# Prompt attention in 32-column tiles, both heads of a pair in one visit

## The chip, the cores and the metric

The kernel runs on one core of a Trainium2 chip. The metric is the device time of one execution in microseconds (us); lower is better. A core has TensorE (PE, with PEld for its weight loads), VectorE (DVE), ScalarE (ACT), GpSimd (POOL) and SyncE (SP), which here issues most DMAs. Matmul results go to PSUM, eight banks in which a [128, 512] fp32 tile fills one; everything else works on SBUF.

## The reference, cut to what matters

One layer of a hybrid decoder, for a prompt of 512 tokens and 8 samples of 4 tokens with the same weights: half a SwiGLU block, a mixer, half a SwiGLU block, a final norm. The mixer projects to queries, keys and values for three dilated attention groups, to a gated convolution and to two gates. What the change touches is the prompt attention, 8 heads of 64 in each group:

```python
GROUPS = ((128, 1), (512, 4), (2048, 16))        # window, dilation
sc = einsum('bdcqhe,bdckhe->bdchqk', qb, kk) * SCALE
sc = where(valid, sc, -inf);  m = max(sc);  p = exp(sc - m);  l = sum(p)
o  = einsum('bdchqk,bdckhe->bdcqhe', p, vv) / l
# the three groups of a head are weighted by a softmax over m + log(l)
```

That weighting equals one softmax over the keys of all three groups together, and so the kernel computes it.

## The kernel before, in words

Activations lie transposed, [128 channels, 544 columns]: 512 prompt and 32 sample tokens in two halves of 272. Each 128x128 weight block is split into a high and a low part in a fast matmul format, so a block is six matmuls into a PSUM tile `mp` (three products, two halves); `run_tiles` walks the tiles and calls `slot` every four blocks, that is every 24 matmuls.

Within a block of 128 query tokens the columns are sorted by token mod 4 into four classes of 32. Group 0 (dilation 1) attends to the same and the previous block (128 columns each); groups 1 and 2 need only keys of the query's own class, 32 per key block.

Work that isn't a projection is put between projection blocks by `slot`: `pe_q` holds generators of which the first gives one step per slot (`v_turn` transposes a value tile, `attention(hp)` does head pair hp), `bg_q` holds convolution steps on VectorE (`ac`, one tap each), given out as long as a planner's clock for VectorE (`clocks`, with the costs of `pe_cost` and `dve_cost`) stays behind that of TensorE. `seq` is the order of the mixer's projections: gated convolution tiles (`gb`, `u`), then q, k, v of one head pair, four times; the attention of a pair is queued when its last value tile is evacuated and runs between the projections of the next pair, the last one between the last four tiles of `seq`.

A step of `attention` before serves one head and one query block: outputs `o` of the step two earlier, transposes `pt` of the probabilities of the step before, scores `s` of its own. The scores of group 0 are matmuls of 64 rows and 128 columns, those of groups 1 and 2 of 64 rows and 32 columns, one per class. Behind them VectorE adds the mask, scales and takes the extreme value (`P<-s,mask`), ScalarE takes the exponential with its sum `L`, TensorE transposes `P`, ScalarE copies to `pT`, and TensorE multiplies with `V`, again full width for group 0 and in 32-column tiles for the others. After both heads `aT` transposes the outputs of a query block back. `S` and `O` are PSUM classes of one bank each, `T` of two, `main` of two tiles of two banks.

Of the kernel before, what the change touches and what calls it, by code (L numbers as in the profile page):

```python
# [23 lines left out]
PACK = [(0, 192), (192, 384), (576, 448), (1024, 512)]  # L24
# [66 lines left out]
def step_kernel(ctx: ExitStack, tc: tile.TileContext, I: dict, O: dict, order: list):  # L91
# [143 lines left out]
    def run_tiles(tiles, lead=1, hooks=None, slack=-500.0):  # L235
# [36 lines left out]
    def v2(t):  # L272
        return t.rearrange("p (h n) -> p h n", h=2)
# [179 lines left out]
    mask = qp.tile([128, 1536], F32, name="mask")  # L453
# [154 lines left out]
    def v_turn(g, hp, t):  # L608
        ps = psum_tile([128, 512], "T", f"vT{g}_{hp}", 2)
        for i in range(4):  # L610
            pe.transpose(ps[:, 128 * i : 128 * i + 128], t[:, 128 * i : 128 * i + 128], ident)
        V[g, hp] = qp.tile([128, 4, 128], F32, tag="V", name=f"V{g}_{hp}", bufs=6)
        act.activation(V[g, hp].rearrange("p a b -> p (a b)"), ps, AF.Copy)
        yield

    def attention(hp):
        units = [(b, h) for b in range(4) for h in range(2)]
        st1, st2 = None, None
        on = {}
        fin = None  # L620
        for step in range(len(units) + 3):
            if fin is not None:
                b = fin
                ps = psum_tile([128, 128], "T", f"aT{hp}_{b}", 2)
                pe.transpose(ps, on[b], ident)
                act.activation(v2(att[hp])[:, b // 2, 128 * (b % 2) : 128 * (b % 2) + 128], ps, AF.Copy)
                fin = None
            if st2 is not None:
                b, h, pT, chunks, L = st2
                o = psum_tile([128, 64], "O", f"o{hp}_{b}_{h}", 1)  # L630
                p0 = 64 * h
                blks = ([b - 1] if b else []) + [b]
                for i, kb in enumerate(blks):
                    pe.matmul(o, pT[:, i, :], V[0, hp][:, kb, p0 : p0 + 64], start=i == 0, stop=False)
                n = 32 * (b + 1)
                for g in (1, 2):
                    ci = len(blks) + g - 1
                    for c in range(4):
                        pe.matmul(o[32 * c : 32 * c + 32, :], pT[:n, ci, 32 * c : 32 * c + 32],
                                  V[g, hp][:n, c, p0 : p0 + 64], start=False, stop=g == 2)  # L640
                if h == 0:
                    on[b] = qp.tile([128, 128], F32, tag="on", name=f"on{hp}_{b}", bufs=2)
                dve.reciprocal(L, L)
                dve.tensor_scalar(out=on[b][:, p0 : p0 + 64], in0=o, scalar1=L, scalar2=None, op0=ALU.mult)
                if h == 1:
                    fin = b
                st2 = None
            if st1 is not None:
                b, h, P, chunks, L = st1
                ps = psum_tile([128, 4, 128], "T", f"pt{hp}_{b}_{h}", 2)  # L650
                pT = qp.tile([128, 4, 128], F32, tag="pT", name=f"pT{hp}_{b}_{h}", bufs=2)
                for i, (off, n) in enumerate(chunks):
                    pe.transpose(ps[:n, i, :], P[:, off : off + n], ident)
                nf = sum(n == 128 for _, n in chunks)
                act.activation(pT[:, :nf], ps[:, :nf], AF.Copy)  # L655
                if nf < len(chunks):
                    n = chunks[-1][1]
                    act.activation(pT[:n, nf : len(chunks)], ps[:n, nf : len(chunks)], AF.Copy)
                st2 = (b, h, pT, chunks, L)
                st1 = None  # L660
            if step < len(units):
                b, h = units[step]
                p0 = 64 * h
                S = psum_tile([128, 512], "S", f"s{hp}_{b}_{h}", 1)
                pos, w = PACK[b]

                def blk(t, kb):
                    return v2(t)[p0 : p0 + 64, kb // 2, 128 * (kb % 2) : 128 * (kb % 2) + 128]

                chunks = []  # L670
                off = 0
                for kb in ([b - 1] if b else []) + [b]:
                    pe.matmul(S[:, off : off + 128], blk(Q[0, hp], b), blk(K[0, hp], kb), start=True, stop=True)
                    chunks.append((off, 128))
                    off += 128
                for g in (1, 2):
                    chunks.append((off, 32 * (b + 1)))
                    for kh in range(b // 2 + 1):
                        nb = min(2, b + 1 - 2 * kh)
                        for c in range(4):  # L680
                            kv = v2(K[g, hp])[p0 : p0 + 64, kh, :256].rearrange("p (b c i) -> p c b i", b=2, c=4)
                            pe.matmul(S[32 * c : 32 * c + 32, off : off + 32 * nb],
                                      blk(Q[g, hp], b)[:, 32 * c : 32 * c + 32], kv[:, c, :nb, :],
                                      start=True, stop=True)
                        off += 32 * nb
                P = qp.tile([128, 512], F32, tag="P", name=f"P{hp}_{b}_{h}", bufs=2)
                mn = qp.tile([128, 1], F32, tag="mn", name=f"mn{hp}_{b}_{h}", bufs=4)
                L = qp.tile([128, 1], F32, tag="L", name=f"L{hp}_{b}_{h}", bufs=4)
                dve.tensor_tensor_reduce(
                    out=P[:, :w], in0=S[:, :w], in1=mask[:, pos : pos + w], scale=-0.125, scalar=BIG,  # L690
                    op0=ALU.add, op1=ALU.min, accum_out=mn)
                act.activation(P[:, :w], P[:, :w], AF.Exp, scale=-1.0, bias=mn, accum_out=L)  # L692
                st1 = (b, h, P, chunks, L)
            yield

# [18 lines left out]
    run_tiles(seq, lead=2, hooks={4: mix_stats})  # L714
# [53 lines left out]
    def sample_keys(hf, res):  # L768
# [8 lines left out]
        S = psum_tile([128, 512], "S", f"sA{hf}", 1)  # L777
# [26 lines left out]
        S = psum_tile([128, 512], "S", f"sB{hf}", 1)  # L804
# [12 lines left out]
    def sample_values(hf, res):  # L817
# [15 lines left out]
        o = psum_tile([128, 512], "O", f"so{hf}", 1)  # L833
# [207 lines left out]
def _constants():  # L1041
# [11 lines left out]
    mask = np.zeros((128, 1536), f)  # L1053
    c, i = np.arange(128) // 32, np.arange(128) % 32
    tok = 4 * i + c
    for b in range(4):
# [5 lines left out]
        n = 32 * (b + 1)  # L1062
# [168 lines left out]
```

## Time and profile before

| | us |
|---|---|
| median of three runs (lowest, highest) | 1498.96 (1498.73, 1500.8) |
| profiled execution | 1497.86 |
| its span | 1496.1 |
| TensorE, VectorE, ScalarE, GpSimd busy | 1467.2, 836.1, 475.4, 320.0 |
| attention of the prompt, first score to last `aT` | 502.4 to 822.0 |

The busy time of TensorE counts overlapping matmuls once; what a piece of work holds of the engine is read from the start of its row to the start of the next one. Line 62 is the helper that records the calls of TensorE, VectorE and GpSimd, so instructions are told apart by their tiles: `mp` the projections, `s`, `pt`, `o`, `aT` the attention, `sA`, `sB`, `so` the sample attention. fp32 matmuls appear as two records each, transposes and `mp` matmuls as one.

### The profile page before, as it was taken

Reading aid. Unit: us, or ns where it says so; the run is one execution under the profiler, and the core shown is the slowest. Engines: PE = TensorE matmul, PEld = TensorE weight load, DVE = VectorE, ACT = ScalarE, POOL = GpSimd, SP = SyncE. Lnnn points to the kernel's source line nnn. Section 1 sums busy time; section 2 is a strip of 40 time slices with the busy share of each in tenths; the row PEclk is TensorE's granted clock in tenths of the full one; section 3 lists DMA queues with packets and bytes.
Section 4 is the critical chain, followed back from the end, with each engine's and each line's share of the span. In section 5 each row is a group of like instructions: output and inputs, shape, how many; then the busy total and the mean of one; then the engine's idle time right before and its main releaser. Section 6 shows DMA issues by size and latency. Waiting matters only on the chain.

```text
span 1496.1 us, 28970 instructions
## 1 busy us (share of the span) xinstructions
PE 1467.2 (98%) x12680; PEld 1418.8 (95%) x12680; DVE 836.1 (56%) x1134; ACT 475.4 (32%) x630; POOL 320.0 (21%) x222
## 2 busy tenths in 40 slices
PE   7999999999999999999999999999999999999996
PEld 7999999999999999999998888789999999999996
DVE  6554445342389879785746866438355544453334
ACT  6222222122353543544444234411332222221221
POOL 1221111101123325332321332103312211110001
PEclk9999999999999999999999999999999999999999
DMA  5444544465598757667572776644443444444331
GB/s 179 183 169 171 181 169 170 178 223 186 175 232 206 171 131 196 143 146 175 124 181 93 263 246 222 201 161 151 149 156 141 142 143 153 142 141 149 133 113 61
DMA packets 63119, 248.67 MB, mean 166 GB/s; under 512 B 8784, under 2 KB 13392, under 8 KB 62160
## 3 DMA queue, kind: packets, MB, share of 16 engines
q1 hardware_dynamic: 54704, 218.71, 41.7%
q0 software_dynamic: 7488, 27.27, 10.9%
q8 instruction: 100, 1.64, 0.4%
q10 hardware_dynamic: 800, 0.84, 0.2%
q14 instruction: 27, 0.22, 0.0%
HBM read 234.21 MB, written 67.10 MB: 201 GB/s over the span
## 4 chain that ended last, share of the span: by engine, by line
PE 92%; DVE 4%; ACT 2%; DMA 1%; issue 0%; POOL 0%; SPq 0%; DVEq 0%; POOLq 0%
PE mp L62 84%; PE s L62 2%; PE o L62 1%; PE mplast L62 1%; PE pt L62 1%; PE so L62 1%; PE sA L62 1%; DVE ga L62 1%; DMA wlo<-in_ws 1%; DVE ac L62 0%; ACT c L927 0%; PE sB L62 0%; PE vT L62 0%; PE st L62 0%; ACT ah L298 0%
## 5 line engine op out<-in xcount | busy, mean ns | idle before, releaser
L62 PE MATMUL mp<-ah,whi 128*128 128x272 f32 x2496 | 526.5, 292 | 6.9 <-ACT whi L166 5.7
L62 PE MATMUL mp<-ah,wlo 128*128 128x272 f32 x2496 | 517.8, 289 | 0.7 <-DMA wlo<-in_ws 0.7
L62 PE MATMUL mp<-al,whi 128*128 128x272 f32 x2496 | 514.6, 287 | 0.1
L62 PEld LDWEIGHTS mp<-ah,whi 128*128 128x128 f32 x2496 | 391.2, 189 | 20.5 <-issue 10.5
L62 PEld LDWEIGHTS mp<-ah,wlo 128*128 128x128 f32 x2496 | 393.7, 189 | 1.3 <-DMA wlo<-in_ws 0.9
L62 PEld LDWEIGHTS mp<-al,whi 128*128 128x128 f32 x2496 | 392.4, 189 | 0.3 <-DVE al L62 0.3
L62 POOL TENSOR_TENSOR wlo<-wraw,whi 128x1024 fp32r<-128x1024 f32 x73 | 177.1, 2427 | 798.4 <-ACT whi L166 488.1
L166 ACT ACTIVATE whi<-wraw 128x1024 fp32r<-128x1024 f32 (+1 forms) x169 | 177.2, 1049 | 346.7 <-PE mp L62 178.4
L62 DVE TENSOR_TENSOR wlo<-wraw,whi 128x1024 fp32r<-128x1024 f32 (+1 forms) x96 | 117.7, 1226 | 221.4 <-ACT whi L166 221.1
L62 DVE SCALAR_TENSOR_TENSOR ac<-u,vec,ac 128x512 f32<-128x512 f32 x232 | 183.3, 848 | 0.0
L348 ACT ACTIVATE ga<-ga 128x544 f32<-128x544 f32 x44 | 29.0, 658 | 237.2 <-DVE ga L62 237.2
L62 DVE TENSOR_TENSOR ga<-ga,mp 128x544 f32<-128x544 f32 x52 | 37.4, 720 | 103.4 <-PE mp L62 101.2
L62 DVE TENSOR_TENSOR ga<-mp,rstd 128x544 f32<-128x544 f32 x52 | 37.6, 724 | 85.5 <-PE mp L62 85.4
L159 ACT ACTIVATE whi<-wraw 128x1024 fp32r<-128x1024 f32 x52 | 54.9, 1055 | 84.4 <-PE mp L62 83.3
L161 POOL DMA_DIRECT2D wlo<-in_ws x52 | 45.6, 877 | 160.6 <-ACT wlo L160 150.9
L160 ACT ACTIVATE wlo<-whi 128x1024 fp32r<-128x1024 f32 x52 | 55.1, 1061 | 1.6
L62 PEld LDWEIGHTS s<-k,q 64*32 64x32 f32 (+1 forms) x880 | 26.1, 117 | 9.9 <-DVE on L62 2.5
L62 DVE CUSTOM_DVE_ANT_0 P<-s,mask 128x192 f32<-128x192 f32 (+3 forms) x32 | 17.7, 554 | 31.3 <-PE s L62 31.2
L62 PE MATMUL s<-k,q 64*32 64x64 f32 (+2 forms) x880 | 34.3, 223 | 0.0
L62 POOL TENSOR_TENSOR q<-q,ra 128x544 f32<-128x544 f32 x12 | 18.6, 1550 | 61.1 <-DVE ra L62 34.7
L692 ACT ACTIVATE P<-P,mn 128x192 f32<-128x192 f32 (+3 forms) x32 | 19.8, 618 | 36.8 <-DVE mn L62 36.7
L62 PE MATMUL o<-V,pT 64*32 64x64 f32 (+4 forms) x624 | 27.5, 230 | 1.0 <-ACT pT L655 1.0
(780 smaller groups left out, 1992.2 us busy)
## 6 DMA issues: line engine op xcount, KB each, us to landing
wraw<-in_ws SPq DMA_DIRECT2D x219, 512.0 KB, 3.4
cache<-in_cache SPq DMA_DIRECT2D x56, 512.0 KB, 4.6
wlo<-in_ws POOLq DMA_DIRECT2D x52, 512.0 KB, 6.3
out_kv<-k SPq DMA_DIRECT2D x12, 272.0 KB, 3.9
out_kv<-vt SPq DMA_DIRECT2D x12, 256.0 KB, 3.9
x<-in_x SPq DMA_DIRECT2D x8, 272.0 KB, 5.6
xkeep<-x SPq DMA_DIRECT2D x8, 272.0 KB, 2.1
xb<-xkeep SPq DMA_DIRECT2D x8, 272.0 KB, 3.3
```

The source lines that it names most:

```text
L62: return f(*a, **kw)
L159: act.activation(whi[u], raw[u], AF.Copy)
L160: act.activation(wlo[u], whi[u].bitcast(F32), AF.Copy, scale=-1.0)
L161: nc.gpsimd.dma_start(wlo[u], I["ws"][u], accum_op=ALU.add)
L166: act.activation(whi[u][:, c], raw[u][:, c], AF.Copy)
L348: act.activation(t, t, AF.Silu)
L692: act.activation(P[:, :w], P[:, :w], AF.Exp, scale=-1.0, bias=mn, accum_out=L)
```

## The change

`attention` now works on both heads of a pair in one step. The scores of all three groups are 64-row, 32-column matmuls; the two heads, which lie in rows 0 to 63 and 64 to 127, alternate, each with its own PSUM tile. Outputs are 32-column matmuls throughout, both heads into one PSUM tile, with one reciprocal and one product. Query blocks 0 and 1 now take 64 keys of groups 1 and 2 (`NCK`, masked beyond the valid ones), so that the two groups fill one operand of 128 rows; a merged value tile `Vm` is made for that by two more copies per pair. Scores of a block stand in one step, the outputs of the block before and the transposes of this one in the next. `S` has two banks and takes the place of `O`. The last four projection tiles of `seq` have a slot every two blocks, and the planner's cost of 32-column matmuls is lower.

```diff
-PACK = [(0, 192), (192, 384), (576, 448), (1024, 512)]
+PACK = [(0, 256), (256, 384), (640, 448), (1088, 512)]
+NCK = [64, 64, 96, 128]
@@ pe_cost
     if out.shape[0] == 32:
-        return (170.0 + 1.5 * n) / 4
+        return max(13.4, 1.67 * n * src.shape[0] / 512)
@@ run_tiles(..., every=4)
-                if k % 4 == 3 or k == n - 1:
+                if k % every == every - 1 or k == n - 1:
                     slot(slack)
@@ v_turn
+        if g:
+            if g == 1:
+                V["m", hp] = qp.tile([128, 4, 128], F32, tag="Vm", name=f"Vm{hp}", bufs=1)
+            r = 64 * (g - 1)
+            act.activation(V["m", hp][r : r + 64].rearrange("p a b -> p (a b)"), ps[:64], AF.Copy)
@@ attention
+        def scores(b):
+            S = [psum_tile([128, 512], "S", f"s{hp}_{b}_{h}", 2) for h in range(2)]
...
+            def tiles(cols, n, g, keys):
+                for c in range(4):
+                    for h in range(2):
+                        r = slice(64 * h, 64 * h + 64)
+                        q0 = HALF * (b // 2) + 128 * (b % 2) + 32 * c
+                        pe.matmul(S[h][32 * c : 32 * c + 32, cols : cols + n], Q[g, hp][r, q0 : q0 + 32],
+                                  keys(K[g, hp][r], c), start=True, stop=True)
...
+            tiles(0, n0, 0, near)
+            off = n0
+            for g in (1, 2):
+                for kh in range(b // 2 + 1):
+                    nb = min(2, NCK[b] // 32 - 2 * kh)
...
+                    tiles(off, 32 * nb, g, far)
+                    off += 32 * nb
+            L[b] = qp.tile([128, 2], F32, tag="L", name=f"L{hp}_{b}", bufs=3)
+            for h in range(2):
...
+                dve.tensor_tensor_reduce(
+                    out=p[:, :w], in0=S[h][:, :w], in1=mask[:, pos : pos + w], scale=-0.125, scalar=BIG,
+                    op0=ALU.add, op1=ALU.min, accum_out=mn)
+                act.activation(p[:, :w], p[:, :w], AF.Exp, scale=-1.0, bias=mn, accum_out=L[b][:, h : h + 1])
...
+        def values(b):
+            o = psum_tile([128, 2, 64], "S", f"o{hp}_{b}", 2)
+            near = [(V[0, hp][:, kb], None) for kb in blocks(b)]
+            far = [(None, V["m", hp])] if NCK[b] == 64 else [(None, V[g, hp]) for g in (1, 2)]
+            parts = near + far
+            for h in range(2):
+                for i, (v, vc) in enumerate(parts):
+                    n = chunks(b)[i][1]
                     for c in range(4):
+                        rhs = (v if vc is None else vc[:n, c])[:, 64 * h : 64 * h + 64]
+                        pe.matmul(o[32 * c : 32 * c + 32, h, :], pT[b, h][:n, i, 32 * c : 32 * c + 32], rhs,
+                                  start=i == 0, stop=i == len(parts) - 1)
...
+        for b in range(6):
+            if b >= 2:
+                final(b - 2)
+            if b < 4:
+                scores(b)
             yield
+            if 1 <= b < 5:
+                values(b - 1)
+            if b < 4:
+                turn(b)
+            if b < 5:
+                yield
@@ behind seq
-    run_tiles(seq, lead=2, hooks={4: mix_stats})
+    run_tiles(seq[:-4], lead=2, hooks={4: mix_stats})
+    run_tiles(seq[-4:], every=2)
@@ sample attention
-        o = psum_tile([128, 512], "O", f"so{hf}", 1)
+        o = psum_tile([128, 512], "S", f"so{hf}", 2)
```

TensorE, first pair, second head of block 0, before: the transposes of the first head (`pt_0_0`), the scores of the second (`s_0_1`), then projection. Shapes are output rows x columns.

```order
L62 MATMUL pt_0_0_5231<-ident,P_0_0_5190 128x128
L62 MATMUL pt_0_0_5231<-ident,P_0_0_5190 32x128 x2
L62 MATMUL s_0_1_5238<-k_0_4532,q_0_4464 128x128
L62 MATMUL s_0_1_5238<-k_0_4747,q_0_4666 32x32 x4
L62 MATMUL s_0_1_5238<-k_0_4967,q_0_4891 32x32 x4
L62 MATMUL mp_5197<-ah_4_3598,whi_5041 128x272 x2
```

The same block's scores after, at the seam between group 0 (`k_0_4532`) and group 1 (`k_0_4747`):

```order
L64 MATMUL s_0_0_5183<-k_0_4532,q_0_4464 32x128
L64 MATMUL s_0_1_5184<-k_0_4532,q_0_4464 32x128
L64 MATMUL s_0_0_5183<-k_0_4747,q_0_4666 32x64
L64 MATMUL s_0_1_5184<-k_0_4747,q_0_4666 32x64
L64 MATMUL s_0_0_5183<-k_0_4747,q_0_4666 32x64
```

The two heads now alternate matmul by matmul, in one tile shape, 24 of them in this block; no transposes stand beside them.

TensorE, first pair, outputs of block 0, before: first head's outputs (`o_0_0`), second head's transposes, first head's scores of block 1.

```order
L62 MATMUL o_0_0_5290<-V_0_4712,pT_0_0_5232 128x64
L62 MATMUL o_0_0_5290<-V_0_4937,pT_0_0_5232 32x64 x4
L62 MATMUL o_0_0_5290<-V_0_5145,pT_0_0_5232 32x64 x4
L62 MATMUL pt_0_1_5303<-ident,P_0_1_5248 128x128
L62 MATMUL pt_0_1_5303<-ident,P_0_1_5248 32x128 x2
L62 MATMUL s_1_0_5310<-k_0_4532,q_0_4464 128x128 x2
L62 MATMUL s_1_0_5310<-k_0_4747,q_0_4666 32x64 x4
L62 MATMUL s_1_0_5310<-k_0_4967,q_0_4891 32x64 x4
```

And after:

```order
L64 MATMUL o_0_5374<-V_0_4712,pT_0_0_5254 32x64 x4
L64 MATMUL o_0_5374<-Vm_4939,pT_0_0_5254 32x64 x4
L64 MATMUL o_0_5374<-V_0_4712,pT_0_1_5259 32x64 x4
L64 MATMUL o_0_5374<-Vm_4939,pT_0_1_5259 32x64 x4
L64 MATMUL pt_1_0_5394<-ident,P_1_0_5331 128x128 x3
L64 MATMUL pt_1_1_5400<-ident,P_1_1_5335 128x128 x3
L64 MATMUL mp_5342<-ah_4_3598,whi_5111 128x272 x2
```

Both heads' outputs stand together, and the transposes behind them are those of the next block, both heads.

ScalarE, last pair, before: the sigmoid of a gate tile (`gb`), weight splits, a value copy, then the first exponential.

```order
L484 ACT_TABLE_LOAD
L484 ACTIVATE gb_8599<-gb_8599 128x544
L159 ACTIVATE whi_8605<-wraw_8488 128x1024
L160 ACTIVATE wlo_8606<-whi_8605 128x1024
L613 ACTIVATE V_3_8641<-vT_3_8636 128x512
L692 ACT_TABLE_LOAD
L692 ACTIVATE P_0_0_8682,L_0_0_8684<-P_0_0_8682,mn_0_0_8683 128x192
```

And after:

```order
L615 ACTIVATE V_3_8664<-vT_3_8659 128x512
L621 ACTIVATE Vm_8515<-vT_3_8659 64x512
L486 ACT_TABLE_LOAD
L486 ACTIVATE gb_8679<-gb_8679 128x544
L675 ACT_TABLE_LOAD
L675 ACTIVATE P_0_0_8710,L_0_8709<-P_0_0_8710,mn_0_0_8711 128x256
L675 ACTIVATE P_0_1_8714,L_0_8709<-P_0_1_8714,mn_0_1_8715 128x256
```

The attention begins one projection tile earlier, so that the two exponentials stand right behind the sigmoid.

## Rows read from the trace of the kernel before

**Rows 1.** The page of the kernel before: span, two engines, the chain by engine.
```profile
span 1496.1 us, 28970 instructions
...
PE 1467.2 (98%) x12680; PEld 1418.8 (95%) x12680; DVE 836.1 (56%) x1134; ACT 475.4 (32%) x630; POOL 320.0 (21%) x222
...
PE 92%; DVE 4%; ACT 2%; DMA 1%; issue 0%; POOL 0%; SPq 0%; DVEq 0%; POOLq 0%
```
**Rows 2.** Windows, second pair's attention: length, busy PE, PEld, DVE, ACT, POOL, clock, DMA.
```profile
600.00:646.00 46.00, 46.00 (x607) 41.87 (x605) 32.93 (x77) 22.00 (x44) 11.92 (x13) 1.00 0.60 134
```
**Rows 3.** PE timeline, first pair, blocks 0 and 1: start, length, instruction, count.
```profile
502.01 0.41 PE L62 MATMUL mp<-al,whi 128*128 128x272 f32 x2
502.35 0.74 PE L62 MATMUL s<-k,q 64*128 64x128 f32 x18
503.02 0.52 PE L62 MATMUL mp<-ah,whi 128*128 128x272 f32 x2
...
510.34 0.69 PE L62 MATMUL o<-V,pT 128*128 128x64 f32 x18
510.96 0.55 PE L62 MATMUL pt<-ident,P 128*128 128x128 f32 x3
511.44 1.07 PE L62 MATMUL s<-k,q 64*128 64x128 f32 x20
512.43 0.52 PE L62 MATMUL mp<-ah,whi 128*128 128x272 f32 x2
```
**Rows 4.** PE timeline, first pair, block 2.
```profile
520.97 0.91 PE L62 MATMUL o<-V,pT 128*128 128x64 f32 x20
521.81 0.65 PE L62 MATMUL pt<-ident,P 128*128 128x128 f32 x4
522.40 1.19 PE L62 MATMUL s<-k,q 64*128 64x128 f32 x36
523.52 0.52 PE L62 MATMUL mp<-ah,whi 128*128 128x272 f32 x2
```
**Rows 5.** PE timeline, last pair, block 3.
```profile
809.93 1.29 PE L62 MATMUL s<-k,q 64*128 64x128 f32 x36
811.15 0.52 PE L62 MATMUL mp<-ah,whi 128*128 128x272 f32 x2
```
**Rows 6.** PE timeline, a visit of the sample attention in 32-column tiles.
```profile
844.83 1.07 PE L62 MATMUL sB<-cache,qbd 128*32 128x512 f32 x8
845.83 0.52 PE L62 MATMUL mp<-ah,whi 128*128 128x272 f32 x2
846.18 0.42 PE L62 MATMUL mp<-ah,wlo 128*128 128x272 f32 x2
846.44 0.42 PE L62 MATMUL mp<-al,whi 128*128 128x272 f32 x2
```
**Rows 7.** PE timeline, end of the last pair; idle time and releaser in brackets.
```profile
820.39 1.02 PE L62 MATMUL o<-V,pT 128*128 128x64 f32 x20 [1.02 <-ACT pT L655]
822.03 0.33 PE L62 MATMUL aT<-ident,on 128*128 128x128 f32 x1 [0.62 <-DVE on L62]
```
**Rows 8.** ACT timeline, first pair, a gate tile's sigmoid between two exponentials.
```profile
511.35 1.28 ACT L484 ACT_TABLE_LOAD   x1 [3.03 <-DVE L L62]
512.64 0.66 ACT L484 ACTIVATE gb<-gb 128x544 f32<-128x544 f32 x1
...
513.74 1.28 ACT L692 ACT_TABLE_LOAD   x1
515.03 0.62 ACT L692 ACTIVATE P<-P,mn 128x384 f32<-128x384 f32 x1
```
**Rows 9.** The tiles s and P: engine, operation, count, duration ns min/median/max.
```profile
L62 PEld LDWEIGHTS s<-k,q x880: 102/107/188, 502.3 to 816.7; 64*32 64x32 f32 x160, 64*128 64x128 f32 x16
...
L62 DVE CUSTOM_DVE_ANT_0 P<-s,mask x32: 331/590/693, 503.5 to 817.0; 128x192 f32<-128x192 f32 x8, 128x384 f32<-128x384 f32 x8, 128x448 f32<-128x448 f32 x8, 128x512 f32<-128x512 f32 x8
L692 ACT ACTIVATE P<-P,mn x32: 456/644/728, 503.9 to 817.8; 128x192 f32<-128x192 f32 x8, 128x384 f32<-128x384 f32 x8, 128x448 f32<-128x448 f32 x8, 128x512 f32<-128x512 f32 x8
```

More of the change, by code (lines that the diff above doesn't have):

```diff
@@ L233, in mm_block, with run_tiles @@
                 )
-    def run_tiles(tiles, lead=1, hooks=None, slack=-500.0):
+    def run_tiles(tiles, lead=1, hooks=None, slack=-500.0, every=4):
         def new():
@@ L452, in step_kernel @@
     sinr = rope_p.tile([128, NTOK], F32, name="sinr")
-    mask = qp.tile([128, 1536], F32, name="mask")
+    mask = qp.tile([128, 1600], F32, name="mask")
     sp.dma_start(cosr, I["rope"][:, 0])
@@ L611, in v_turn @@
             pe.transpose(ps[:, 128 * i : 128 * i + 128], t[:, 128 * i : 128 * i + 128], ident)
[L612 removed]
+        V[g, hp] = qp.tile([128, 4, 128], F32, tag="V", name=f"V{g}_{hp}", bufs=5)
         act.activation(V[g, hp].rearrange("p a b -> p (a b)"), ps, AF.Copy)
+        if g:
[3 more added lines that the diff above has]
+            act.activation(V["m", hp][r : r + 64].rearrange("p a b -> p (a b)"), ps[:64], AF.Copy)
@@ L614, in v_turn @@
         yield
     def attention(hp):
[L617 to L637, printed above, removed]
-                    for c in range(4):
[L639 to L693, printed above, removed]
-            yield
@@ new lines, in attention, with blocks, chunks, near @@
+        P, pT, L, on = {}, {}, {}, {}
+        def blocks(b):
+            return ([b - 1] if b else []) + [b]
+        def chunks(b):
+            o = 128 * len(blocks(b))
+            r = [(128 * i, 128) for i in range(len(blocks(b)))]
+            n = NCK[b]
+            return r + ([(o, 2 * n)] if n == 64 else [(o, n), (o + n, n)])
+        def scores(b):
+            S = [psum_tile([128, 512], "S", f"s{hp}_{b}_{h}", 2) for h in range(2)]
+            pos, w = PACK[b]
+            n0 = 128 * len(blocks(b))
+            def tiles(cols, n, g, keys):
[5 more added lines that the diff above has]
+                                  keys(K[g, hp][r], c), start=True, stop=True)
+            def near(k, c):
+                if b == 2:
+                    return k[:, 128:416].rearrange("p (a n) -> p a n", a=2)[:, :, :128]
+                k0 = HALF * (b // 2)
+                return k[:, k0 : k0 + n0]
+            tiles(0, n0, 0, near)
[3 more added lines that the diff above has]
+                    nb = min(2, NCK[b] // 32 - 2 * kh)
+                    def far(k, c):
+                        return v2(k)[:, kh, :256].rearrange("p (b c i) -> p c b i", b=2, c=4)[:, c, :nb, :]
+                    tiles(off, 32 * nb, g, far)
+                    off += 32 * nb
+            L[b] = qp.tile([128, 2], F32, tag="L", name=f"L{hp}_{b}", bufs=3)
+            for h in range(2):
+                p = P[b, h] = qp.tile([128, 512], F32, tag="P", name=f"P{hp}_{b}_{h}", bufs=2)
+                mn = qp.tile([128, 1], F32, tag="mn", name=f"mn{hp}_{b}_{h}", bufs=4)
+                dve.tensor_tensor_reduce(
+                    out=p[:, :w], in0=S[h][:, :w], in1=mask[:, pos : pos + w], scale=-0.125, scalar=BIG,
+                    op0=ALU.add, op1=ALU.min, accum_out=mn)
+                act.activation(p[:, :w], p[:, :w], AF.Exp, scale=-1.0, bias=mn, accum_out=L[b][:, h : h + 1])
@@ new lines, in turn @@
+        def turn(b):
+            for h in range(2):
+                ps = psum_tile([128, 4, 128], "T", f"pt{hp}_{b}_{h}", 2)
+                t = pT[b, h] = qp.tile([128, 4, 128], F32, tag="pT", name=f"pT{hp}_{b}_{h}", bufs=2)
+                for i, (off, n) in enumerate(chunks(b)):
+                    pe.transpose(ps[:n, i, :], P[b, h][:, off : off + n], ident)
+                nf = sum(n == 128 for _, n in chunks(b))
+                act.activation(t[:, :nf], ps[:, :nf], AF.Copy)
+                if nf < len(chunks(b)):
+                    n = chunks(b)[-1][1]
+                    act.activation(t[:n, nf : len(chunks(b))], ps[:n, nf : len(chunks(b))], AF.Copy)
@@ new lines, in values @@
+        def values(b):
[3 more added lines that the diff above has]
+            parts = near + far
+            for h in range(2):
+                for i, (v, vc) in enumerate(parts):
+                    n = chunks(b)[i][1]
+                    for c in range(4):
+                        rhs = (v if vc is None else vc[:n, c])[:, 64 * h : 64 * h + 64]
+                        pe.matmul(o[32 * c : 32 * c + 32, h, :], pT[b, h][:n, i, 32 * c : 32 * c + 32], rhs,
+                                  start=i == 0, stop=i == len(parts) - 1)
+            dve.reciprocal(L[b], L[b])
+            on[b] = qp.tile([128, 128], F32, tag="on", name=f"on{hp}_{b}", bufs=2)
+            dve.tensor_tensor(out=on[b].rearrange("p (h e) -> p h e", h=2), in0=o,
+                              in1=L[b].unsqueeze(2).to_broadcast([128, 2, 64]), op=ALU.mult)
@@ new lines, in final @@
+        def final(b):
+            ps = psum_tile([128, 128], "T", f"aT{hp}_{b}", 2)
+            pe.transpose(ps, on[b], ident)
+            act.activation(v2(att[hp])[:, b // 2, 128 * (b % 2) : 128 * (b % 2) + 128], ps, AF.Copy)
+        for b in range(6):
[3 more added lines that the diff above has]
+                scores(b)
+            yield
+            if 1 <= b < 5:
[4 more added lines that the diff above has]
+                yield
```

8 lines of the change are left out of this document (4 added, 4 removed).

## The prediction

> **What bounds the kernel now.** I read the page first. TensorE is busy for 1467 of 1496 us and the chain that ended last lies on it for 92%, while VectorE is busy for 56% [rows 1]; so a microsecond taken from TensorE's own queue is a microsecond of the end, as long as nothing else becomes late. The second view is the stretch of one head pair's attention: TensorE is busy for all of its 46 us, its weight loads for 41.87, VectorE for 32.93, and the granted clock is 1.00, that is 2.4 GHz [rows 2]. The third view is TensorE's timeline there. The attention stands in small visits between groups of 24 matmuls of the input projection (`mp`), and the difference between the start of a row and the start of the next one is what the visit holds of the engine; the length in the row is longer, since matmuls overlap. By this measure a score visit of one head costs 0.67 us for query block 0 and 0.99 for block 1 [rows 3], 1.12 for block 2 [rows 4] and 1.22 for block 3 [rows 5]; an output visit 0.62 for block 0 [rows 3] and 0.84 for the others [rows 4]; three transposes 0.48 [rows 3], four 0.59 [rows 4].
>
> **What a 32-column tile costs.** Each fp32 matmul is two records (a visit of 1 + 8 matmuls counts x18). Block 3 has 16 records with 64 columns more than block 1 and takes 0.23 us more (1.22 less 0.99): 0.014 us a record. Block 2 has 16 records with 32 columns more and takes 0.13 more: 0.008 a record, so there the pace of issue counts and not the columns [rows 3 to 5]. The sample attention has 8 records of 512 columns in 1.00 us [rows 6]; at 0.014 for 64 columns these are 0.90, which leaves 0.10 for leaving the shape. The next `mp` pair then takes 0.35 instead of 0.26 [rows 6], and a visit that begins behind `mp` starts 0.08 late (502.27 would be plain, 502.35 it is) [rows 3]. So a visit in another tile shape pays about 0.3 us beside its contents. A transpose is 0.11 (0.59 less 0.48).
>
> The Trainium skill (TensorE: Matmul & The Clock Gate, Part 3: Packing small matmuls) holds that a weight load overlaps matmuls in flight only when their row groups differ. All value tiles of this change have the same row group; by that rule each of their 832 records would pay a load of its own, which I price below as a rival. The trace disagrees: 16 such records and two full ones stand in 0.62 us [rows 3].
>
> **The change, one head pair, step by step.**
> Before: scores 2 x (0.67 + 0.99 + 1.12 + 1.22) = 8.00; outputs 2 x 0.62 + 6 x 0.84 = 6.28; transposes 2 x 0.48 + 6 x 0.59 = 4.50; eight returns from scores to `mp` at 0.10 = 0.80. Sum 19.6 us.
> After, scores: one visit per block for both heads, all in 64-row, 32-column tiles. Counted in records of 64 columns, block 0 has 64, block 1 96, block 2 96 plus 32 of 32 columns, block 3 128. One half after the other this is 0.90 + 1.34 + (1.34 + 0.25) + 1.79 = 5.62 us. If the two row halves stream side by side, all but the 0.25 halves: 2.94. The trace never uses both halves at once, so these are two bounds; a third, further out below, is the pace of issue alone (256 records x 0.008 = 2.0), and above, a drain at every change of half (rivals). I take 2.94: four column groups do stream side by side in rows 3 to 6, the two heads write two PSUM tiles, and nothing in the rows sets rows apart from columns. With four visits at 0.3: 4.1.
> The same page's section on packing gives 10.6 times for 16 tiles in rows and columns; no run here shows it, and by it the sum would be the 2.94 taken, with the serial bound gone.
> After, outputs: blocks 0 and 1 put both dilated groups into one operand of 128 rows, so the parts per head are 2, 3, 4, 4; times two heads, four columns and two records these are 208 records of 64 columns, 2.9 us. They leave for transposes, not for `mp`; with 0.25 for each of four changes: 3.9.
> After, transposes: 26 instead of 30, 2.86, plus 0.1 for four returns to `mp`: 3.3. The four final transposes stay, but two of them now return to `mp`: 0.2.
> Sum after 11.5; difference 8.1 a pair, 32.2 for four pairs.
>
> **The end of the last pair.** Today its last steps run with no `mp` left between them, and TensorE idles 1.02 and 0.62 us there [rows 7]. The new call gives the last four projection tiles a step every two blocks instead of four, so all 11 steps find cover: 1.6 us saved.
>
> **What is late next.** Both heads' masks and exponentials now follow one visit. The longest take 0.69 on VectorE and 0.73 on ScalarE [rows 9]. The second head's probabilities are ready after 0.1 + 0.69 + 2 x 0.83 = 2.4 us; with 24 `mp` matmuls (3.0 us) between, this is hidden in pairs 0 to 2. In pair 3 there are 12 (1.5 us) plus the output visit (0.65 to 1.1): about even, I allow 0.6 us for a queue on either engine. Two places are worse. A gate tile (`gb`) evacuated just ahead of an exponential needs two table loads: from 510.34, where its matmuls ended, to the exponential at 515.03 are 4.7 us [rows 3, 8], 4.15 without the two copies between. In pair 3 block 0 the same order now meets a visit 2.2 us later: the first head's probabilities come at about 4.7, the second's at 5.3, and TensorE stands 2.9 us. In pair 0 block 1 TensorE arrives at 4.6: 0.5 us. New stalls: 4.0, between 0 and 8. The instructions queued behind such a late exponential on ScalarE are the splits `whi`, `wlo` of the weights two tiles ahead, 12 us away, so they stay hidden.
>
> Other edits cost nothing on TensorE: 8 copies into `Vm` are ScalarE's, which is busy 22 of 46 us [rows 2]; on VectorE 32 reciprocals and 32 products become 16 and 16; a smaller PSUM class is gone, but a score bank of block b+1 waits only for outputs that the final transpose ahead of it waits for anyway. The lower costs in the planner move at most a dozen convolution steps later, and all are caught up before the gate tiles.
>
> **Sum.** 32.2 + 1.6 - 4.0 = 29.8 us. The profiled execution took 1497.9 (1.8 around its span); the median is 1.1 above it. 1499.0 - 29.8 = 1469 us.
>
> **Rivals.**
> 1. The row halves stream one after the other: 4 x 2.68 = 10.7 more, 1480 us. For it: no row shows two halves at once. Against it: column groups do.
> 2. The shorter cover bites in every block of pair 3, and the planner's lower costs make VectorE late: stalls of 8 to 12 us instead of 4, 1475. For it: 1.5 us steps against chains of 2.4. Against it: only 8 of 44 steps are of that kind.
> 3. VectorE becomes the bound of the attention stretches and the time comes back as waits: 1499. It works 32.9 of 46 us [rows 2]; in 38 us that is 87%, still under the span.
> 4. The slower side: each change between the row halves drains the array as a change of tile shape does. The scores have 4 x 256 = 1024 records whose halves alternate; at the 0.08 to 0.1 us of rows 3 and 6 this is 80 to 100 us, 1560. It decides from 0.029 us a record on. Against it: column groups alternate at 0.014 with their work included.
> 5. Every value record pays its weight load: at the 0.107 us of rows 9, 832 x 0.107 = 89 instead of 11.6, 1546. Rows 3 exclude it in this shape, so it gets one in a hundred.
>
> **How the numbers follow.** The forecast has 0.62, rival 1 0.17, rival 2 0.12, rival 3 0.03, rival 4 0.05, rival 5 0.01. The forecast's own range: issue pace alone (-4) and no stalls (-4) give 1461, 8 us of stalls 1473. Reaching to rival 1 with its spread gives 1461 to 1483, which leaves out about 0.15. A difference under 0.2% (3 us) cannot be told from none. Faster: 0.91; no change: rival 3, 0.03; slower: rivals 4 and 5, 0.06.
>
> **What would show it.** In the timeline after: score visits of 0.5, 0.75, 1.0 and 1.0 us to the next row (0.95 to 1.9 if the halves follow one another), output visits of 0.5 to 1.0 us, 104 transposes, no idle row before the last output, and idle of some 2.5 us ahead of the first transposes of the last pair with ScalarE's table load as the cause. The forecast is wrong if score visits last as long as two of today's, or if `mp` pairs inside the pairs wait for VectorE.

## The result, and the profile after

| | before | after |
|---|---|---|
| median, us | 1499.59 (1498.73 to 1500.8, 4 runs) | 1474.3 (1473.93 to 1475.0, 4 runs) |
| profiled execution, its span, us | 1497.86, 1496.1 | 1475.0, 1473.2 |

The ratio is 0.984 with a 95% interval of 0.9826 to 0.9854. The forecast was 1469 with a range of 1461 to 1483: the sign and the range hold, the gain is 25.3 us (22.9 between the two profiled executions) where 29.8 were worked out. One execution of the run with the later start, below, took 7962.01 us; its median there is with it, its range without.

The page of the changed kernel, beside [rows 1]: TensorE is still the engine that bounds, and the chain still lies on it for 91%.

```profile
span 1473.2 us, 29595 instructions
...
PE 1439.8 (98%) x13016; PEld 1398.4 (95%) x13016; DVE 833.0 (57%) x1102; ACT 471.0 (32%) x620; POOL 319.1 (22%) x222
...
PE 91%; DVE 4%; ACT 2%; DMA 1%; issue 1%; SPq 0%; DVEq 0%; ACTq 0%
```

The stretch of [rows 2], as windows (length, busy PE, PEld, DVE, ACT, POOL, granted clock, DMA share, GB/s). Its 46 us hold 724 matmul records instead of 607, at the same clock.

```profile
600.00:646.00 46.00, 46.00 (x724) 43.95 (x723) 32.18 (x73) 21.20 (x39) 16.66 (x19) 1.00 0.67 155
```

TensorE's timeline in the first pair, beside [rows 3, 4]: score visits of blocks 0, 1, 2 and 3, each with the row behind it, and two later visits: the outputs of block 0 with the transposes of block 1, and the outputs of block 2 with the transposes of block 3.

```profile
503.69 0.83 PE L64 MATMUL s<-k,q 64*32 64x128 f32 x48
504.45 0.52 PE L64 MATMUL mp<-ah,whi 128*128 128x272 f32 x2
...
511.10 1.04 PE L64 MATMUL s<-k,q 64*32 64x256 f32 x48
512.08 0.52 PE L64 MATMUL mp<-ah,whi 128*128 128x272 f32 x2
...
515.28 0.32 PE L64 MATMUL o<-V,pT 128*32 128x64 f32 x8
...
516.04 1.15 PE L64 MATMUL pt<-ident,P 128*128 128x128 f32 x6
516.94 0.50 PE L64 MATMUL mp<-ah,whi 128*128 128x272 f32 x2
...
520.25 1.26 PE L64 MATMUL s<-k,q 64*32 64x256 f32 x80
521.44 0.52 PE L64 MATMUL mp<-ah,whi 128*128 128x272 f32 x2
...
529.60 1.36 PE L64 MATMUL s<-k,q 64*32 64x256 f32 x80
530.88 0.52 PE L64 MATMUL mp<-ah,whi 128*128 128x272 f32 x2
...
534.10 1.11 PE L64 MATMUL o<-V,pT 128*32 128x64 f32 x64
535.13 1.09 PE L64 MATMUL pt<-ident,P 128*128 128x128 f32 x8
535.98 0.49 PE L64 MATMUL mp<-ah,whi 128*128 128x272 f32 x2
```

A visit of both heads now holds TensorE for 0.76, 0.98, 1.19 and 1.28 us in blocks 0 to 3, where one head alone held it for 0.67, 0.99, 1.12 and 1.22 [rows 3 to 5]. So a visit of two heads costs hardly more than one of one head did. The outputs of both heads in block 2 take 1.03 us.

Then the last pair. Here TensorE stands twice, which the kernel before did not do at these places; the two idle rows of [rows 7] are gone.

```profile
752.17 0.41 PE L64 MATMUL mp<-al,whi 128*128 128x272 f32 x2
754.88 0.93 PE L64 MATMUL pt<-ident,P 128*128 128x128 f32 x4 [2.30 <-ACT P L675]
755.57 0.57 PE L64 MATMUL mp<-ah,whi 128*128 128x272 f32 x2
...
787.07 0.41 PE L64 MATMUL mp<-al,whi 128*128 128x272 f32 x2
791.25 0.79 PE L64 MATMUL mp<-ah,whi 128*128 128x272 f32 x2 [3.77 <-DVE us L64]
```

The first stop, 2.30 us, is the one that the prediction placed in pair 3, block 0. ScalarE's rows beside [rows 8]: sigmoid, table load, and only then the first exponential.

```profile
750.96 1.28 ACT L486 ACT_TABLE_LOAD   x1 [1.10 <-DVE gb L64]
752.26 0.66 ACT L486 ACTIVATE gb<-gb 128x544 f32<-128x544 f32 x1
752.93 1.28 ACT L675 ACT_TABLE_LOAD   x1
754.23 0.51 ACT L675 ACTIVATE P<-P,mn 128x256 f32<-128x256 f32 x1
```

The second, 3.77 us, was not foreseen. TensorE waits for VectorE to empty the last gated tile (`u`, `us`). VectorE's timeline shows six convolution taps ahead of it, 9.41 us in all:

```profile
780.69 9.41 DVE L64 SCALAR_TENSOR_TENSOR ac<-u,vec,ac 128x512 f32<-128x512 f32 x6
...
790.06 1.01 DVE L64 TENSOR_TENSOR u<-mp,gb 128x256 f32<-128x256 f32 x2
790.93 0.17 DVE L64 TENSOR_TENSOR us<-mp,gb 128x32 f32<-128x32 f32 x1
```

The median tap of the kernel takes 0.743 us; of these six the shortest takes 0.739 and the longest 2.87 (tile `ac`, durations in ns min/median/max, here of 780.6 to 790):

```profile
L64 DVE SCALAR_TENSOR_TENSOR ac<-u,vec,ac x6: 739/1302/2873, 780.7 to 789.4; 128x512 f32<-128x512 f32 x6
```

GpSimd's timeline of the same time holds three instructions:

```profile
780.64 1.36 POOL L64 TENSOR_TENSOR gb<-gb,rstd 128x544 f32<-128x544 f32 x1 [9.12 <-ACT gb L486]
781.96 2.84 POOL L64 TENSOR_TENSOR wlo<-wraw,whi 128x1024 fp32r<-128x1024 f32 x1
786.41 2.48 POOL L64 TENSOR_TENSOR wlo<-wraw,whi 128x1024 fp32r<-128x1024 f32 x1 [1.61 <-ACT whi L168]
```

They end at 782.00, 784.80 and 788.89. VectorE's single records put the ends of three taps at 782.55, 785.35 and 789.44, each 0.55 us behind; the other three take 0.74. So each of the three long taps looks like one that waited until a GpSimd instruction was done, and not like one that ran slower beside it.

What the stops leave behind is in the windows (columns as above). The granted clock falls to 0.50, that is 1.2 GHz, once 2.3 us without a matmul have passed, and again within the 3.8 us:

```profile
754.00:756.00 2.00, 1.06 (x7) 0.82 (x8) 0.36 (x4) 1.99 (x6) 0.00 (x0) 0.96 0.00 0
756.00:758.00 2.00, 2.00 (x11) 2.00 (x10) 0.00 (x0) 1.87 (x4) 0.35 (x1) 0.50 0.36 70
758.00:760.00 2.00, 2.00 (x52) 1.24 (x52) 0.05 (x1) 0.00 (x0) 0.51 (x1) 0.68 0.85 231
...
790.00:792.00 2.00, 0.75 (x3) 0.78 (x4) 2.00 (x7) 0.00 (x0) 0.00 (x0) 0.50 0.01 2
...
796.00:798.00 2.00, 2.00 (x15) 2.00 (x15) 2.00 (x4) 0.18 (x1) 0.00 (x0) 0.80 0.89 248
```

### The profile page after: what moved, and what is told of

Read it like the earlier page. It is cut to its first block, busy times and chain, and to the rows that moved or that the text cites. A ratio compares the mean times of both kernels' runs of the same rounds, so it can differ in the third digit from the quotient of the medians.

```text
span 1473.2 us, 29595 instructions
## 1 busy us (share of the span) xinstructions
PE 1439.8 (98%) x13016; PEld 1398.4 (95%) x13016; DVE 833.0 (57%) x1102; ACT 471.0 (32%) x620; POOL 319.1 (22%) x222
## 3 DMA queue, kind: packets, MB, share of 16 engines
q0 software_dynamic: 7488, 27.27, 10.9%
## 4 chain that ended last, share of the span: by engine, by line
PE 91%; DVE 4%; ACT 2%; DMA 1%; issue 1%; SPq 0%; DVEq 0%; ACTq 0%
PE mp L64 84%; PE mplast L64 1%; DMA wlo<-in_ws 1%; PE s L64 1%; PE so L64 1%; PE o L64 1%; PE pt L64 1%; PE sA L64 1%; DVE ga L64 1%; DVE ac L64 1%; ACT c L956 0%; PE vT L64 0%; PE sB L64 0%; PE st L64 0%; ACT ah L300 0%
## 5 line engine op out<-in xcount | busy, mean ns | idle before, releaser
L64 DVE SCALAR_TENSOR_TENSOR ac<-u,vec,ac 128x512 f32<-128x512 f32 x232 | 189.2, 876 | 0.0
L675 ACT ACTIVATE P<-P,mn 128x256 f32<-128x256 f32 (+3 forms) x32 | 19.9, 623 | 34.5 <-DVE mn L64 34.5
L64 POOL TENSOR_TENSOR k<-k,ra 128x544 f32<-128x544 f32 x12 | 19.3, 1606 | 36.6 <-DVE ra L64 33.0
L64 DVE TENSOR_TENSOR dn<-mp,rstd 128x544 f32<-128x544 f32 x15 | 10.8, 720 | 24.9 <-PE mp L64 24.9
L64 DVE TENSOR_TENSOR gc<-gc,mp 128x544 f32<-128x544 f32 x8 | 5.8, 721 | 32.1 <-PE mp L64 32.1
L64 DVE TENSOR_TENSOR ssum<-ssum,sq 128x544 f32<-128x544 f32 x27 | 21.4, 793 | 4.5 <-ACT sq L311 4.4
```

The costliest lines, as they stand in the source:

```text
L64: return f(*a, **kw)
L675: act.activation(p[:, :w], p[:, :w], AF.Exp, scale=-1.0, bias=mn, accum_out=L[b][:, h : h + 1])
```

## The experiments

All are edits of the changed kernel, and their ratios are to the kernel before on the same chip (medians 1499.05, 1499.09 and 1498.17 in these batches).

**Do the row halves stream side by side?** One run lets both heads read rows 0 to 63; the second head's scores are left out by that.

```diff
-                        r = slice(64 * h, 64 * h + 64)
+                        r = slice(0, 64)
```

> The second head is left out: both heads' score matmuls read rows 0 to 63, so the number of records, their columns, their order and the two PSUM tiles stay, and only the two row halves coincide. If the halves stream side by side (read from the changed kernel's trace, bursts of eight records per 56 ns), each score visit must grow by the half that no longer overlaps: at most 2.7 us a pair, less what the pace of issue (17 ns a record behind the 32nd) already costs, so some 2.0 to 2.5 us a pair and 8 to 10 us in all, about 1483 us; visits of 1.1, 1.5, 1.8 and 2.0 us instead of 0.76, 0.98, 1.19 and 1.29. Rival (the gain comes from one tile shape and fewer shape changes, the halves add nothing): the visits and the time stay, 1474 us.

1482.11 us (1480.78 to 1483.56), ratio 0.9886 (0.9871 to 0.9901). TensorE's timeline, first pair, block 0:

```profile
504.31 1.14 PE L64 MATMUL s<-k,q 64*32 64x128 f32 x48
505.38 0.52 PE L64 MATMUL mp<-ah,whi 128*128 128x272 f32 x2
```

The same visit holds TensorE for 1.07 us instead of 0.76; block 3, read in the same way, for 1.96 instead of 1.28. So in the changed kernel the two halves do stream side by side, and that is worth 7.8 us. Added up over the score visits of all four pairs, start to next row, TensorE is held for 32.1 us before, 25.5 in this run and 17.3 in the changed kernel: the one shape and the joint visit bring 6.6 us, the two halves 8.2. The run also bears on the rule of the Trainium skill that the prediction weighed (TensorE: Matmul & The Clock Gate, Part 3: Packing small matmuls; weight loads overlap only across row groups): 48 loads one after another at the 0.107 us of [rows 9] would be 5.1 us for this visit, and it takes 1.07 with all its records in the same rows, so the trace disagrees.

**The closer steps of the last four tiles.** One run takes them back:

```diff
-    run_tiles(seq[:-4], lead=2, hooks={4: mix_stats})
-    run_tiles(seq[-4:], every=2)
+    run_tiles(seq, lead=2, hooks={4: mix_stats})
```

> Undoes one part: the last four projection tiles have a slot every four blocks again. Theory: the two stops of TensorE in the last pair, 2.3 us for the first exponential and 3.8 us for the late evacuation of u, and the half clock that follows each (2.0 and 2.8 us by the profile after), come from the halved distance of the steps. Without it they go (-10.8), the uncovered end comes back (+1.7) and a gate's sigmoid costs 0.5 in block 1: about 1465.5 us, and no half clock before the sample attention. Rival (as the prediction counted it: the closer steps save 1.6 and cost 2.9, the evacuation is late for another reason): 1473 us, or 1476 where the uncovered end weighs more.

1468.72 us (1464.78 to 1469.34), ratio 0.9791 (0.9776 to 0.9806). Both stops are gone. A new one stands at the end of the last pair, with its stretch at 1.2 GHz: the last transpose of an output waits for `on`, and `on` for five taps, one of which again waits for GpSimd (`wlo` at 787.18, 2.38 us).

```profile
793.29 0.33 PE L64 MATMUL aT<-ident,on 128*128 128x128 f32 x1 [2.36 <-DVE on L64]
```

VectorE's timeline there:

```profile
788.07 0.29 DVE L64 TENSOR_TENSOR on<-o,L 128x128 f32<-128x128 f32 x1 [1.46 <-PE o L64]
788.28 4.48 DVE L64 SCALAR_TENSOR_TENSOR ac<-u,vec,ac 128x512 f32<-128x512 f32 x5
...
792.94 0.29 DVE L64 TENSOR_TENSOR on<-o,L 128x128 f32<-128x128 f32 x1
```

The closer steps cost 5.6 us here; the prediction had them save 1.6, against a stop of 2.9 that it placed in the same pair.

**Fewer taps ahead of the last gated tile.**

```diff
-    run_tiles(seq[-4:], every=2)
+    run_tiles(seq[-4:-1], every=2)
+    run_tiles(seq[-1:], every=2, slack=-4000.0)
```

> In the last of the four tiles VectorE is granted fewer convolution taps ahead of the evacuation of u (1 instead of 6 by the order); all else as in the changed kernel. Theory (the evacuation is late because six taps, slowed beside GpSimd, stand ahead of it on VectorE): the stop of 3.8 us and its half clock of 2.8 go, about 1468 us, the first stop of 2.3 stays. Rival (the evacuation waits for the sigmoid or the scaled gate, not for taps): the stop stays and so does the time, 1474 us; second rival (the taps deferred make the layer norm late): the wait ahead of the convolution output grows from 2.3 by up to 5 us and the gain is lost.

1473.07 us (1472.23 to 1475.11), ratio 0.9824 (0.9807 to 0.984). One tap instead of six stands ahead of `u`, and the stop of 3.77 us is gone. The gain is not: further on TensorE now waits 6.24 us instead of 2.34 for the first operand after the layer norm (`cs0h`). The layer norm needs all taps, but they aren't later here: the last one ends at 853.8 (854.7 in the changed kernel). The operand comes at 922.4 (922.6), while TensorE is there 4 us earlier. TensorE's timeline, the changed kernel first, then this run:

```profile
923.19 0.79 PE L64 MATMUL mp<-cs0h,whi 128*128 128x272 f32 x2 [2.34 <-DVE cs0h L64]
...
922.96 0.79 PE L64 MATMUL mp<-cs0h,whi 128*128 128x272 f32 x2 [6.24 <-DVE cs0h L64]
```

The first stop is 2.30 us here too, as expected, but the clock doesn't fall behind it (windows as above; the matmuls begin again at 755.60):

```profile
756.00:758.00 2.00, 1.94 (x20) 1.75 (x20) 0.00 (x0) 1.97 (x4) 0.00 (x0) 1.00 0.00 0
```

**The last pair two slots later.**

```diff
-                pe_q.append((tick["n"] + 4, attention(hp)))
+                pe_q.append((tick["n"] + (6 if hp == 3 else 4), attention(hp)))
```

> The last pair's attention starts two slots (24 matmuls) later, so that 12 projection matmuls stand between the gate tile and the first scores. Theory (the first stop is the chain of table load, sigmoid, table load and two exponentials behind the gate tile, 5.2 us long): the stop falls from 2.3 to about 1.0 and its half clock goes, the late u stays: about 1471 us. Rival (the half clock comes from the low activity of 32-column visits two blocks apart, not from the stop): the half clock stays, 1473 us.

1470.49 us (1469.17 to 1470.62), ratio 0.9805 (0.9789 to 0.9822): the time that was expected, not for the reason given. The first stop did not shrink; it is 2.86 us, since two weight splits came between sigmoid and exponential on ScalarE. The granted clock behind it is 0.50 from 756 to 760, so the half clock stays, as the rival has it; what brings it is not settled by that. The late `u` is what went.

```profile
750.89 0.66 ACT L486 ACTIVATE gb<-gb 128x544 f32<-128x544 f32 x1
751.46 1.05 ACT L161 ACTIVATE whi<-wraw 128x1024 fp32r<-128x1024 f32 x1
...
753.61 1.28 ACT L675 ACT_TABLE_LOAD   x1
754.91 0.51 ACT L675 ACTIVATE P<-P,mn 128x256 f32<-128x256 f32 x1
```

**GpSimd's part in the long taps.** The gate scale and three weight splits of that stretch go from GpSimd to VectorE, in the same order; the planner's own clocks are left as if GpSimd did them.

```diff
+    def swapped(n):
+        if either(n) is dve:
+            return dve
+        clocks["pool"] = max(clocks["pe"] - 3000.0, clocks["pool"]) + pool_cost(None, None, None, n)
+        return nc.vector
...
-                (dve if u < 3 else either(n)).tensor_tensor(
+                (dve if u < 3 else swapped(n) if U_GATES <= u < U_GATES + 3 else either(n)).tensor_tensor(
...
-                either(NTOK).tensor_tensor(out=t, in0=t, in1=norm["rstd"], op=ALU.mult)
+                (swapped if len(cbuf) >= 5 else either)(NTOK).tensor_tensor(out=t, in0=t, in1=norm["rstd"], op=ALU.mult)
```

> As the changed kernel with the same order and the same taps on VectorE, but the four elementwise instructions that GpSimd runs around the late evacuation of u (a gate scaling and three weight splits) run on VectorE. Theory (the six taps ahead of the evacuation take 9.4 us instead of 4.4 because GpSimd works beside them): they fall to 4.5 us, and although VectorE has some 2 us more to do ahead of u and must wait for the sigmoid, u comes about 2 us earlier; the stop of 3.8 us shrinks to about 1.5, 1471 us. Rival (the queue's length alone makes u late): the taps still take 9 us, the stop grows to about 6 us, 1477 us.

1468.98 us (1468.07 to 1471.42), ratio 0.9799 (0.9784 to 0.9814). The same six taps now take 4.06 us, and the stop for `u` is gone:

```profile
780.83 4.06 DVE L64 SCALAR_TENSOR_TENSOR ac<-u,vec,ac 128x512 f32<-128x512 f32 x6
784.84 0.59 DVE L64 TENSOR_TENSOR u<-mp,gb 128x256 f32<-128x256 f32 x1
```

With the records above this settles why `u` was late: VectorE had the time for the six taps, and lost 5.35 us of it to three GpSimd instructions. A smaller stop is new (1.53 us before an `aT`; VectorE now waits itself for the sigmoid). The first stop is still 2.3 us, yet no stretch at 1.2 GHz follows it, as in the run with fewer taps; so part of the gain of 5.3 us may be the clock. In windows as above:

```profile
754.00:756.00 2.00, 1.95 (x16) 1.72 (x14) 0.00 (x0) 1.97 (x4) 0.00 (x0) 1.00 0.00 0
```

**The planner's lower costs** of 32-column matmuls, taken back:

```diff
-        return max(13.4, 1.67 * n * src.shape[0] / 512)
+        return (170.0 + 1.5 * n) / 4
```

> Undoes the planner's lower cost of 32-column matmuls alone. By the order, the convolution taps of the pairs before move by at most a dozen places and those ahead of the last u evacuation are 7 instead of 6. Theory (this cost only moves taps): the same stops and visits, 1474 us within 2. Rival (the lower cost left a backlog of taps that makes u late): the stop of 3.8 us shrinks or goes, 1468 us.

1476.66 us (1474.79 to 1477.34), ratio 0.9846 (0.9831 to 0.986). Slower by 2 us if anything: stops of 2.30, 0.76 and 4.31 us stand in the last pair. So the lower costs are not what put the taps in front of `u`.

**Why the score visits are longer than the forecast's.** The starts of the 48 records of the first visit (block 0, at 503.69), as distances in ns to the next start:

```
  7   6   7   7   6   7   7  86   7   7   6   7   7   6   7  62
  7   7   6   7   7   6   7   9   7   7   6   7   7   6   7   9
 76   8  17  17  16  17  11   6  10   6  11  17  16  17  17
```

The first 32 come in groups of eight, one group's starts within 50 ns. Behind the 33rd is a pause of 76 ns, and from there they come one by one, 13 ns apart in the mean. In all 16 score visits a pause of 75 or 76 ns stands at this place; the records behind it come 9 to 13 ns apart in the mean. In block 0 those behind are the narrow ones of group 2, so a narrow matmul or the place in the visit could be the reason. This run puts the narrow ones first:

```diff
-            tiles(0, n0, 0, near)
             off = n0
...
+            tiles(0, n0, 0, near)
             L[b] = qp.tile([128, 2], F32, tag="L", name=f"L{hp}_{b}", bufs=3)
```

> In each score visit the narrow matmuls of groups 1 and 2 go first and the wide ones of group 0 last; all else as in the changed kernel. Theory (the first 32 records of a visit start 7 ns apart, those behind them 12 to 17 ns, whatever they are): the wide records, which stream longer than that, hide the slow pace; visits fall from 0.76 to about 0.61, 0.98 to 0.83, 1.19 to 1.12, 1.29 to 1.2, in all 1.5 us, 1472.5 us. Rival (the slow pace belongs to the narrow matmuls of group 2 themselves): visits within 0.05 of those before, 1474 us.

1474.9 us (1473.82 to 1475.96), ratio 0.9836 (0.9821 to 0.9851): no gain. The visits hold 0.76, 0.98, 1.29 and 1.29 us. The pause (64 ns) stands behind the 33rd record of the first visit here too, and the wide records behind it start 17 ns apart in the mean. So the pause goes with the place and not with the width. The Trainium skill (TensorE: Matmul & The Clock Gate, Part 3, The mechanism) states that TensorE pulls weight loads ahead of matmuls in flight, within a window 64 deep. 32 matmuls and their 32 loads would be 64, and the trace is near that; it is no proof, since in the run with both heads in the same rows only 28 ns stand behind the 33rd record of the first visit. No run took the window itself away, and what sets the pace behind the pause isn't shown.

**The two edits together**, steps every four blocks and narrow ones first:

> Slots every four blocks in the last tiles and narrow scores first, together. Theory: 1468.7 less 1.5 is about 1467 us. Rival (the layer norm's wait ahead of the convolution output takes back what TensorE gains earlier): 1468.5 us with that wait grown from 1.7 to about 3 us.

1467.5 us (1465.82 to 1468.09), ratio 0.9783 (0.9767 to 0.9799). The lowest median of all, though not to be told from the run with the steps alone.

**The remaining stop of that version.** The taps are held back until the last outputs are copied (steps every four blocks as well):

```diff
+            if hp == 3 and b == 3:
+                bg_when["n"] = tick["n"] + 4
```

> Undoes the closer steps of the last four projection tiles and holds the convolution taps of the last pair's third block back from VectorE until the last outputs are copied. Theory (the stop is VectorE's taps standing ahead of the copies that the final transposes wait for): the 2.4 us stop near 791 falls to 1.2 or less, the half clock behind it goes, 1465.5 us. Rival (VectorE has no slack left for the taps themselves): the held taps come later, the layer norm's wait ahead of the sample attention grows from 1.7 to about 4 us, 1468.5 us.

1467.91 us (1467.81 to 1470.63), ratio 0.9793 (0.9779 to 0.9808). The stop falls from 2.36 to 0.41 us and the clock stays at 1.00 there, as the theory has it; the time stays too, since the wait for `cs0h` grows from 1.74 to 6.26 us, as the rival has it.

```profile
790.90 0.33 PE L64 MATMUL aT<-ident,on 128*128 128x128 f32 x1 [0.41 <-DVE on L64]
...
918.47 0.79 PE L64 MATMUL mp<-cs0h,whi 128*128 128x272 f32 x2 [6.26 <-DVE cs0h L64]
```

But not for the rival's reason: the last tap ends earlier (849.3 against 852.5), and TensorE reaches `cs0h` 3.8 us earlier (912.2 against 916.05), yet the operand comes at 918 as before. In this run the layer norm itself meets GpSimd: one of its sums on VectorE (`lnacc`, 0.73 us each in the changed kernel) takes 2.12 us and ends 0.58 us behind a weight split. A row of GpSimd's timeline, then one of VectorE's:

```profile
875.36 2.90 POOL L64 TENSOR_TENSOR wlo<-wraw,whi 128x1024 fp32r<-128x1024 f32 x1 [9.23 <-ACT whi L168]
...
876.72 2.12 DVE L64 TENSOR_TENSOR lnacc<-lnacc,lnsq 128x544 f32<-128x544 f32 x1 [0.72 <-ACT lnsq L939]
```

**The held taps without GpSimd's part:**

> As the run before, and the four GpSimd instructions beside those taps are on VectorE. Theory (GpSimd beside VectorE's taps makes each tap about twice as long): six taps take some 4.1 us, not 9; layer norm wait no longer than 2.4, 1464.5 us. Rival (VectorE has four more instructions, and they wait for the sigmoid): no gain over the run before, or 1467 us.

1471.09 us (1469.54 to 1474.31), ratio 0.9816 (0.9799 to 0.9834). Four taps take 2.73 us where they took 4.26, and it gains nothing: the wait for `cs0h` is 6.26 us again, and a stop of 1.33 us before the transposes of block 1 is new.

## Why the forecast was right, and where it was not

The measured 1474.3 us lies in the stated range, but not in the forecast's own, which ended at 1473 (8 us of stalls); the range reached further only to take in rival 1, which the runs exclude. That it held is in part luck, and the time is the one that rival 2 gave.

I counted TensorE's records from the first transpose of a value tile (461.73 before, 462.31 after) to the first matmul on `cs0h` (945.66 and 923.19). A visit is its start to the next start, plus what the `mp` intervals at its sides exceed 0.125 us. Stretches at 1.2 GHz, and the 0.45 us by which the outputs and transposes at 515.28 are longer than in other pairs, are taken out and stand in rows of their own.

| term, four pairs, us | forecast | measured |
|---|---|---|
| scores | 35.2 to 16.4: 18.8 | 35.8 to 19.4: 16.4 |
| outputs | 25.1 to 15.6: 9.5 | 25.7 to 16.2: 9.5 |
| transposes | 18.0 to 13.2: 4.8 | 17.4 to 12.3: 5.1 |
| `aT` returns | -0.8 | -0.7 |
| end of the last pair | 1.6 | 1.65 |
| stops | -4.0 | -6.5 (2.30, 3.77, 0.45) |
| clock at 1.2 GHz | none | -2.8 (4.4 after, 1.6 before) |
| sum | 29.9 | 22.7 |

The clock's 4.4 are worked out from the timeline: 24 `mp` matmuls from 791.25 to 796.82 take 5.57 us instead of 3.0, and the visits and matmuls from 754.88 to 759.75 take 1.85 us more than the same ones at full clock. The 1.6 before are 16 `mp` matmuls that take 3.62 us instead of 2.0, from 840.12 to 843.74 at a granted clock of 0.57, behind the small `sA` matmuls; the changed kernel has no such stretch there. A window of the kernel before:

```profile
840.00:842.00 2.00, 2.00 (x12) 2.00 (x12) 1.64 (x6) 0.00 (x0) 0.00 (x0) 0.57 0.98 381
```

Nothing shown ties that stretch to the change: of the twelve profiles here six have one behind the `sA` matmuls and six have none; of the two with steps every four blocks and untouched taps, one has it. So of the clock's row only the 4.4 can be put down to the change. The time from the first of these records to the last went from 483.93 to 460.88 us, 23.1 less, so 0.4 us is in none of the rows.

- **What bounds, and the visits**: right. The removed work comes to 30.3 us of the 32.2. Rivals 1, 4 and 5 are excluded by the visits, and the first by experiment: 0.76 us for 48 score records leaves no room for halves one by one or for a drain per change (80 us in all), and 1.03 us for 64 output records none for a load per record.
- **Scores, 3.0 us too low**: the bound that I took lets all records stream at the pace of eight tiles. Only the first 33 of a visit do. The term is mis-sized, and its mechanism is right. Its reading that records of 32 columns go by the pace of issue was not borne out by its rows either: 0.008 us is about half of 0.014, as the columns have it.
- **Closer steps, the step that failed**: "The new call gives the last four projection tiles a step every two blocks instead of four, so all 11 steps find cover: 1.6 us saved." They find cover, and 1.65 were saved there. But with them the last pair meets a late exponential with 12 matmuls as cover (2.30, forecast 2.9) and the late `u` (3.77), and in the profiled execution pays the clock for both, a term that the prediction put at nothing. Taking the part back gains 5.6 us.
- **The planner's costs**: "move at most a dozen convolution steps later, and all are caught up before the gate tiles" fell at the second half: six taps stood ahead of the last gated tile, and were late by 5.35 us through GpSimd. Old costs did not help, so the blame that rival 2 puts on the lower ones is false, though its size is what came (stalls of 8 to 12 us and 1475; the stops and the clock behind them are 10.9). The Trainium skill has the rule that I should have weighed (SBUF - State Buffer, SBUF: two separate sides): VectorE, in an instruction with two SBUF inputs, and a GpSimd instruction that reads SBUF exclude each other for the whole instruction. The trace agrees, with three taps that end 0.55 us behind GpSimd. [Rows 2] showed both engines busy and I read them as independent.
- **Rival 3** (VectorE as the bound): false as a whole, since in the stretch of [rows 2] VectorE is busy for 32.18 of 46 us and TensorE for all of them; in the last pair it was late for the reason above.

What is left open: the versions that remove a stop in the last pair give the time back at the layer norm. In the profiles before, after, with steps every four blocks and with held taps, the first matmul on `cs0h` starts at 945.66, 923.19, 917.79 and 918.47, and from there to the end of the span it is 550.4, 550.0, 549.4 and 550.4. All of the difference lies ahead of that matmul, and its operand no longer follows TensorE alone. The traces show the path. In the three runs with a wait of 6.24 or 6.26 us (fewer taps, held taps, held taps without GpSimd's part) the chain that ended last leaves TensorE some 47 us before `cs0h` (871.09 to 918.47 with held taps) and runs through the layer norm on VectorE, ScalarE and GpSimd, with the weight split shown above on it; in the changed kernel it leaves TensorE only at 896.20. No run took that split away, so how much of the wait is its own isn't shown.

## What to carry to other kernels

When two matrices of half the rows wait for one array, issue them alternately into different row halves and PSUM tiles: the second came at little cost here (1.28 us for both, 1.96 with both in the same half). Price such a visit in two parts, since only its first 33 records streamed at the full pace here. And before closer steps are given to a stretch, list what VectorE and GpSimd run there side by side and who waits for VectorE: an order with slack on paper had none when three of six instructions waited for the other engine.

## What the runs showed of the hardware that was not expected

- Score records in eight tiles of the array start 7 ns apart within groups of eight up to the 33rd of a visit; behind it, after a pause of 76 ns, 9 to 13 ns apart in the mean, and wide ones of 128 columns 17.
- A convolution tap on VectorE that meets a GpSimd instruction ends 0.55 us behind it: 1.86, 2.87 and 2.85 us instead of 0.74.
- A stop of 2.30 us was followed by a granted clock of 0.50 for 3 us in the changed kernel, and by none in two others, without GpSimd's instructions and with fewer taps, where the same stop stands at the same place; the second has the same program up to there. So the stop alone doesn't decide it. What else does, these runs don't show.
